# mLSTM decay matrices: the mask from TensorE to GpSimd, the column terms from TensorE to ScalarE's bias

## The chip, the core and the metric

The kernel runs on one core of a Trainium2 chip. A core has five engines that work side by side, each through its own queue of instructions in order: TensorE (PE, matrix products; its weight loads are listed as PEld), VectorE (DVE), ScalarE (ACT), GpSimd (POOL) and SyncE (SP, which here only issues loads and stores). They meet by semaphores. Matrix products write to PSUM, which has eight banks; everything else lies in SBUF. POOL works on SBUF alone. The metric is the time on the device of one execution, in microseconds (us); lower is better.

## The reference, cut to what matters

The reference is one block of a backbone network: a modulation, an input projection whose columns go to four mixers (an mLSTM in both directions, a gated MLP in chunks, a convolution, a state-space scan), an output projection, a layer norm, a SwiGLU feed-forward part and a second layer norm, for 1024 tokens of width 1024 with 256 context tokens. The change touches the mLSTM mixer alone. In a chunk, and for each head and direction, that one computes

```python
logw = jnp.where(lower, b[..., :, None] - b[..., None, :] + ic[..., None, :], -jnp.inf)
m_t = jnp.maximum(inter, jnp.max(logw, axis=-1))
s = jnp.einsum('bhtd,bhsd->bhts', qc, kc) * jnp.exp(logw - m_t[..., None])
num = jnp.einsum('bhts,bhsd->bhtd', s, vc) + w_inter[..., None] * jnp.einsum('bhvk,bhtk->bhtv', C, qc)
```

The factor `exp(logw - m_t)` is the decay matrix. Its exponent is a term that belongs to the later token t, plus a term that belongs to the earlier token s, where s is not after t; elsewhere the factor is zero. In the backward direction the order of the tokens is turned round.

## The kernel before, in words

The kernel is written with a tile framework: the program is traced as Python, and a list scheduler orders the instructions of each engine by its own model of their durations, with the order of tracing as the rank. It puts instructions of a lower rank where it thinks that an engine has nothing else to do. Buffers come from pools with a fixed count for each tag, and an instruction that needs a new buffer waits until an old one is released. On the chip each engine follows the order it was given.

All large products (`projT` and `projK` at L877 and L889, the output projection at L1184, the feed-forward part at L1345 and L1470) are made of three passes in a reduced fp32 format (`fp32r`) with operands that are split into a high and a low part: ACT casts the high part (L854) and DVE makes the remainder (L855).

The mLSTM uses chunks of 128 tokens: 8 for the latent stream and 2 for the context. It has these steps:

- `mlstm_gates` (L374) works on rows that stand for direction, head and chunk: 40 rows for the forward direction from partition 0 and 40 for the backward one from partition 64, each with 128 tokens along the columns. It makes the running sum `b`, the term of the earlier token `av`, its running maximum `A`, the factors of the states and of the denominators (`Q`, transposed at L468 and exponentiated into `G.TW` at L471), and the operands of the decay matrices: `G.R` (`mR`, L463), the row terms -A, spread over four heads, and `G.AL` (`mAL`, L460), the column terms, both as high and low part.
- `mlstm_states` (L475) makes the states of all chunks.
- `mlstm_chunk` (L522) is traced for the chunks 0 to 3 at L1101 and for 4 to 7 at L1135. For each it makes the scores (L531) in two PSUM banks of tag `a`, and for each direction a decay matrix of 128 tokens by 4 heads x 128 tokens: three matmuls into one bank of tag `b` (two buffers), of which the first adds the mask (identity times a table of 0 and -1e30, L538), the second the row terms (`sel1` picks the chunk, L539), and the third the column terms (`sel2` spreads them over a head's columns, L541). ACT takes the exponential of the whole bank into a tile of tag `mD` (L544; three buffers, shared with two other tiles). DVE multiplies it with the scores, half by half (L548), and PE takes the product with the values (L564), again into tag `b`. The rest (L554 to L578) adds the part from the states and divides.
- `mlstm_norm` (L581) is the norm behind it.

While the chunks run, PE's queue holds matmuls of projections (L884, and in the second group L1184 of the output projection's first half) between the short ones, and DVE's queue holds taps of the convolution (`conv_taps`, L675 and L681) and sums of the late modulation (L968). POOL has memsets and a few loads (L1127 and L1128 for the gated MLP's tables). The table of constants `cst` (L756) is loaded once at the start (L840), and L1064 and L1065 cast the identity, `sel1`, `sel2` and both masks into `fp32r`.

Of the kernel before, what the change touches and what calls it, by code (L numbers as in the profile page):

```python
# [9 lines left out]
F32 = mybir.dt.float32  # L10
F32R = mybir.dt.float32r
I32 = mybir.dt.int32
AF = mybir.ActivationFunctionType
ALU = mybir.AluOpType
MUL, ADD, SUB, MAX, MIN = ALU.mult, ALU.add, ALU.subtract, ALU.max, ALU.min
# [4 lines left out]
def bc(ap, shape):  # L20
    return ap.to_broadcast(shape)
# [327 lines left out]
NEG = -1.0e30  # L349
HO = (0, 2, 1, 3)  # L350


def mlstm_consts():

    sel1 = np.zeros((128, 10), np.float32)
    sel2 = np.zeros((128, 40), np.float32)
    dl = np.zeros((128, 4), np.float32)
    rst = np.zeros((128, 104), np.float32)
    for b in (0, 64):
        for h in range(4):  # L360
            for i in range(10):
                r = b + h * 10 + i
                sel1[r, i] = 1
                sel2[r, i * 4 + HO.index(h)] = 1
                dl[r, HO.index(h)] = 1
                if i == 0:
                    rst[:, r] = NEG
    p = np.arange(128)
    mf = np.where(p[:, None] <= p[None, :], 0, NEG).astype(np.float32)
    mb = np.where(p[:, None] >= p[None, :], 0, NEG).astype(np.float32)  # L370
    return {"sel1": sel1, "sel2": sel2, "dl4": dl, "rst": rst, "maskf": mf, "maskb": mb}


def mlstm_gates(e, Gk, page, kp):  # L374

    nc = e.nc
    v, a, pe = nc.vector, nc.scalar, nc.tensor
    G = Env()
    N = 104
# [7 lines left out]
    ps = e.ps("b")  # L387
    for k in range(2):
        for d in range(2):
            pe.matmul(ps[d * 64:d * 64 + 40, k * 128:(k + 1) * 128], lhsT=Gt[:, k, d].rearrange("p h c -> p (h c)"),  # L390
                      rhs=e.ident, start=True, stop=True)
# [48 lines left out]
    nc.gpsimd.memset(Q, 0.0)  # L440
    hl = kp.tile([128, 4, 128], F32R, name="mhl", tag="mD", bufs=3)
    hi, lo, nh, nl = (hl[0:N, i] for i in range(4))
    v.tensor_copy(hi, av)
    v.tensor_tensor(lo, av, hi.bitcast(F32), op=SUB)
    v.tensor_scalar(nh, A, -1.0, None, op0=MUL)
    v.scalar_tensor_tensor(nl, A, -1.0, nh.bitcast(F32), op0=MUL, op1=SUB)
    G.AL, G.R = [], []
    for d in range(2):
        q = slice(d * 64, d * 64 + 40)
        R = (lambda x: x) if d == 0 else (lambda x: x[:, ::-1])  # L450
        v.tensor_scalar(R(Q[q, 0]), av[q], col[q, 0:1], None, op0=ADD)
        v.tensor_scalar(R(Q[q, 1]), A[q], -1.0, col[q, 1:2], op0=MUL, op1=ADD)
        v.scalar_tensor_tensor(R(Q[q, 2]), b[q], -1.0, A[q], op0=MUL, op1=SUB)
        AL = kp.tile([128, 128], F32R, name=f"mAL{d}")
        RR = kp.tile([128, 4, 128], F32R, name=f"mR{d}")
        nc.gpsimd.memset(AL.bitcast(F32), 0.0)
        nc.gpsimd.memset(RR.bitcast(F32), 0.0)
        for x, (s1, s2) in enumerate(((hi, nh), (lo, nl))):
            o = slice(x * 64, x * 64 + 40)
            v.tensor_copy(R(AL[o]), s1[q].bitcast(F32))  # L460
            src = s2[q].bitcast(F32)
            src = src if d == 0 else src[:, ::-1]
            v.tensor_tensor(RR[o], bc(src[:, None, :], [40, 4, 128]), bc(e.dl4[q, :, None], [40, 4, 128]), op=MUL)  # L463
        G.AL.append(AL)
        G.R.append(RR)
    ps = e.ps("b")
    for i in range(3):
        pe.transpose(ps[:, i * N:(i + 1) * N], Q[0:N, i], e.ident[0:N, 0:N])  # L468
    G.TW = kp.tile([128, 3, 2, 40], F32, name="mTW")
# [52 lines left out]
def mlstm_chunk(e, G, c, qT, kT, vx, hb, wp):  # L522
# [10 lines left out]
    D = []  # L533
    for d in range(2):
        i = step(d)
        ps = e.ps("b")
        m = e.mask[:, d, None, :]
        pe.matmul(ps, lhsT=e.identr, rhs=bc(m, [128, 4, 128]), start=True, stop=False)  # L538
        pe.matmul(ps, lhsT=bc(e.sel1[0:104, i:i + 1], [104, 128]), rhs=G.R[d][0:104].rearrange("p h t -> p (h t)"),  # L539
                  start=False, stop=False)  # L540
        pe.matmul(ps, lhsT=G.AL[d][0:104], rhs=bc(e.sel2[0:104, i * 4:i * 4 + 4, None], [104, 4, 128]),  # L541
                  start=False, stop=True)
        D.append(wp.tile([128, 4, 128], F32, name="mD", tag="mD", bufs=3))
        a.activation(D[d].rearrange("p h t -> p (h t)"), ps, AF.Exp)  # L544
    for d in range(2):
# [138 lines left out]
def conv_norm(e, x, y, q, lnw, lnb, wp):  # L684
# [16 lines left out]
    for j in range(2):  # L701
# [9 lines left out]
CST = (("ident", 128), ("jrow", 160), ("dl16", 16), ("dl4", 4), ("rst", 104),  # L711
       ("sel1", 10), ("sel2", 40), ("maskf", 128), ("maskb", 128))

# [49 lines left out]
def body(tc, A, out):  # L763
# [5 lines left out]
    with st:  # L769
# [292 lines left out]
        mp = tc.alloc_tile_pool(name="mixers", bufs=1, side="right", reuse_waits="tile")  # L1062
        cr = mp.tile([128, 434], F32R, name="cr")
        v.tensor_copy(cr[:, 0:128], e.ident)  # L1064
        v.tensor_copy(cr[:, 128:434], cst[:, off["sel1"].start:off["maskb"].stop])  # L1065
        e.identr, e.sel1, e.sel2 = cr[:, 0:128], cr[:, 128:138], cr[:, 138:178]
        e.mask = cr[:, 178:434].rearrange("p (d t) -> p d t", d=2)
        G = mlstm_gates(e, Gk, mp.tile([128, 2080], F32, name="mC", tag="mC"), mp)
# [504 lines left out]
```

## Time and profile before

| | |
|---|---|
| median of 3 runs | 1174.7 us (1173.6 to 1176.86) |
| profiled execution | 1174.02 us, its span 1172.2 us |
| mean granted TensorE clock | 0.989 |
| busy: PE, DVE, ACT, POOL | 97%, 79%, 38%, 1% of the span |
| HBM traffic | 136.54 MB read, 40.35 MB written |

The profile is of one execution. In a row of a group stand the line of the program, the engine, the operation, the tile written and the tiles read, the shape, the count, the busy time in us with the mean duration of one in ns, and the idle time of the engine just before, with what ended it. In a row of a timeline the first two columns are start and length in us, and a bracket holds the idle time before it. Ends of matmuls are modelled, since they are pipelined, so the distance between two starts says more than the length of one. The granted clock is the share of its full clock that TensorE got.

### The profile page before, as it was taken

The numbers are of one execution on the slowest core, as the hardware profiler recorded it, in microseconds if no ns is written. First come the engines' busy times: TensorE is split into PE (matmuls) and PEld (weight loads), VectorE is DVE, ScalarE is ACT, GpSimd is POOL, SyncE is SP. The second block draws the span as 40 slices with busy tenths as digits, with TensorE's granted clock in tenths as the row PEclk, the third lists the DMA queues.
The fourth block names the chain that finished last, engine by engine and source line by source line (L and its number), as shares of the span: only waits on it lengthen the run. The fifth ranks groups of instructions, "written<-read, shape, count | busy, mean of one in ns | idle before, by whom it ended". The sixth has DMA issues, their size and how long they took to land.

```text
span 1172.2 us, 15295 instructions
## 1 busy us (share of the span) xinstructions
PE 1133.1 (97%) x5671; PEld 895.4 (76%) x5671; DVE 930.0 (79%) x1851; ACT 445.6 (38%) x691; POOL 9.6 (1%) x30
## 2 busy tenths in 40 slices
PE   6999999999999999989999999999999999999996
PEld 1487788667888788868887888888887778888884
DVE  6588999978899889879968676777778767766775
ACT  1454444522326433582233332333232336433431
POOL 0010000000000000000000000000000000000000
PEclk9999999999999999999999999999999999999998
DMA  9542111022143346362333545345445679766621
GB/s 359 212 133 89 42 46 57 27 71 70 57 141 109 99 157 212 99 225 73 108 123 112 196 179 180 134 153 192 170 154 202 255 259 349 238 196 220 195 103 72
DMA packets 63147, 177.87 MB, mean 152 GB/s; under 512 B 5537, under 2 KB 9793, under 8 KB 61282
## 3 DMA queue, kind: packets, MB, share of 16 engines
q1 hardware_dynamic: 62658, 175.93, 43.3%
q8 instruction: 44, 0.72, 0.3%
q0 software_dynamic: 272, 0.70, 0.2%
q10 hardware_dynamic: 144, 0.29, 0.1%
q14 instruction: 29, 0.24, 0.1%
HBM read 136.54 MB, written 40.35 MB: 151 GB/s over the span
## 4 chain that ended last, share of the span: by engine, by line
PE 77%; DVE 13%; DMA 4%; issue 4%; ACT 2%; POOL 0%; DVEq 0%; ACTq 0%; POOLq 0%
PE mm L1345 16%; PE mm L884 13%; PE a L1345 8%; PE mm L1470 6%; PE mm L1184 4%; PE b L1345 4%; PE b L884 4%; PE a L1470 3%; PE b L1470 3%; PE mm L893 3%; PE c L1470 2%; PE b L564 1%; DVE whl L855 1%; DVE pg L855 1%; DMA raw<-in_w_dram 1%
## 5 line engine op out<-in xcount | busy, mean ns | idle before, releaser
L854 ACT CAST whl<-raw 128x512 fp32r<-128x512 f32 (+1 forms) x198 | 120.3, 622 | 283.2 <-PE mm L884 69.6
L884 PE MATMUL mm<-pg,whl 128*128 128x512 f32 x816 | 217.7, 406 | 1.4 <-ACT pg L1207 1.2
L1345 PE MATMUL mm<-pg,whl 128*128 128x512 f32 x864 | 205.9, 390 | 0.4 <-DVE whl L855 0.3
L1345 PEld LDWEIGHTS mm<-pg,whl 128*128 128x128 f32 x864 | 161.9, 188 | 35.6 <-issue 0.8
L884 PEld LDWEIGHTS mm<-pg,whl 128*128 128x128 f32 x816 | 147.7, 190 | 38.8 <-issue 6.1
L855 DVE TENSOR_TENSOR whl<-raw,whl 128x512 fp32r<-128x512 f32 (+1 forms) x198 | 133.6, 689 | 46.3 <-ACT whl L854 44.7
L1345 PE MATMUL a<-pg,whl 128*128 128x512 f32 x432 | 104.7, 390 | 3.6 <-ACT whl L854 3.6
L1345 PEld LDWEIGHTS a<-pg,whl 128*128 128x128 f32 x432 | 80.7, 188 | 21.3 <-ACT whl L854 4.8
L855 DVE TENSOR_TENSOR pg<-raw,pg 128x1024 fp32r<-128x1024 f32 (+1 forms) x52 | 59.6, 1149 | 20.8 <-ACT pg L854 20.7
L855 DVE TENSOR_TENSOR pg<-whl,pg 128x1024 fp32r<-128x1024 f32 (+1 forms) x42 | 47.4, 1133 | 31.9 <-ACT pg L854 31.6
L854 ACT CAST pg<-raw 128x1024 fp32r<-128x1024 f32 (+1 forms) x52 | 51.5, 992 | 48.9 <-DMA raw<-in_w_dram 18.0
L854 ACT CAST pg<-whl 128x1024 fp32r<-128x1024 f32 (+1 forms) x42 | 41.1, 980 | 65.9 <-PE c L1470 25.2
L893 PE MATMUL mm<-whl,pg 128*128 128x256 f32 (+1 forms) x448 | 63.1, 288 | 0.0
L893 PEld LDWEIGHTS mm<-whl,pg 128*128 128x128 f32 x448 | 58.1, 190 | 1.5 <-issue 1.1
L1345 PE MATMUL b<-pg,whl 128*128 128x512 f32 x216 | 51.9, 389 | 0.0
L1184 PE MATMUL mm<-pg 128*128 128x512 f32 x192 | 50.8, 409 | 0.0
L1184 PE MATMUL mm<-whl,pg 128*128 128x512 f32 x192 | 50.2, 398 | 0.3 <-DVE pg L1172 0.3
L1470 PE MATMUL mm<-pg,pg 128*128 128x512 f32 x171 | 48.0, 389 | 0.0
L1470 PE MATMUL a<-pg,pg 128*128 128x512 f32 x162 | 47.2, 390 | 0.2 <-DVE hs L1484 0.2
L1470 PE MATMUL b<-pg,pg 128*128 128x512 f32 x162 | 47.1, 389 | 0.0
L1345 PEld LDWEIGHTS b<-pg,whl 128*128 128x128 f32 x216 | 40.5, 188 | 8.4
L1184 PEld LDWEIGHTS mm<-pg 128*128 128x128 f32 x192 | 37.4, 198 | 8.6 <-DVE pg L855 0.7
(468 smaller groups left out, 1838.2 us busy)
## 6 DMA issues: line engine op xcount, KB each, us to landing
raw<-in_w_dram SPq DMA_DIRECT2D x59, 512.0 KB
gd<-pg SPq DMA_DIRECT2D x22, 1024.0 KB
whl<-gd SPq DMA_DIRECT2D x35, 512.0 KB
pg<-in_w2k_dram SPq DMA_DIRECT2D x11, 1024.0 KB
td<-pg SPq DMA_DIRECT2D x11, 1024.0 KB
raw<-td SPq DMA_DIRECT2D x20, 512.0 KB
pg<-in_wm_dram SPq DMA_DIRECT2D x16, 512.0 KB
raw<-in_wo_dram SPq DMA_DIRECT2D x16, 512.0 KB
```

Of the source, the lines that this page charges most:

```text
L564: pe.matmul(ps[:, x * 65:(x + 1) * 65], lhsT=D[d][:, x], rhs=vx[:, h, :], start=True, stop=True)
L854: a.copy(hi, r)
L855: v.tensor_tensor(lo, r, hi.bitcast(F32), op=SUB)
L884: pe.matmul(ps[h], lhsT=W(wi, k), rhs=rhs(hi, h, k), **f)
L893: pe.matmul(ps, lhsT=lhs(hi, k), rhs=Ws[k // 4](wi, k % 4), start=(k == 0 and n == 0), stop=(k == 7 and n == 2))
L1184: pe.matmul(ps, lhsT=Yr(hi, half, k)[:, t * 128:(t + 1) * 128], rhs=Ws[k // 2](wi, k % 2), start=(i + n == 0), stop=(i == 7 and n == 2))
L1345: pe.matmul(ps, lhsT=W[:, wi, k, :], rhs=B[b][hi][:, k], start=(first and k + n == 0), stop=(k == 3 and n == 2), skip_group_check=True)
L1470: pe.matmul(ps[t], lhsT=Ag[:, hi, k, t * 128:(t + 1) * 128], rhs=Bg[:, wi, k], start=(first and k0 + k + m == 0), stop=(k0 + k == NK - 1 a ...
```

## The change

The mask and the column terms leave TensorE. The kernel after keeps one matmul for a decay matrix, that of the row terms. `mlstm_gates` no longer makes the split column terms; it turns `av` back into the order of the tokens, in the place of the gate inputs (`IF`), transposes it with the three others, and copies the result into `G.a`, where the tokens stand on partitions. In `mlstm_chunk` ACT takes the exponential for each head by itself, 128 columns with the head's column of `G.a` as bias. Then POOL's `affine_select` goes over the whole matrix in place, and puts zero where the earlier token is not before or at the later one. The tables `sel2`, `maskf` and `maskb` go from the constants, and with them the casts.

```diff
-    hl = kp.tile([128, 4, 128], F32R, name="mhl", tag="mD", bufs=3)
-    hi, lo, nh, nl = (hl[0:N, i] for i in range(4))
-    v.tensor_copy(hi, av)
-    v.tensor_tensor(lo, av, hi.bitcast(F32), op=SUB)
+    hl = kp.tile([128, 2, 128], F32R, name="mhl", tag="mD", bufs=3)
+    nh, nl = (hl[0:N, i] for i in range(2))
...
-        AL = kp.tile([128, 128], F32R, name=f"mAL{d}")
+        v.tensor_copy(R(IF[q, 0]), av[q])
         RR = kp.tile([128, 4, 128], F32R, name=f"mR{d}")
-        nc.gpsimd.memset(AL.bitcast(F32), 0.0)
         nc.gpsimd.memset(RR.bitcast(F32), 0.0)
-        for x, (s1, s2) in enumerate(((hi, nh), (lo, nl))):
+        for x, s2 in enumerate((nh, nl)):
             o = slice(x * 64, x * 64 + 40)
-            v.tensor_copy(R(AL[o]), s1[q].bitcast(F32))
...
-    for i in range(3):
-        pe.transpose(ps[:, i * N:(i + 1) * N], Q[0:N, i], e.ident[0:N, 0:N])
+    for i in range(4):
+        pe.transpose(ps[:, i * N:(i + 1) * N], Q[0:N, i] if i < 3 else IF[0:N, 0], e.ident[0:N, 0:N])
+    G.a = kp.tile([128, 2, 40], F32, name="mAL")
+    for d in range(2):
+        v.tensor_copy(G.a[:, d], ps[:, 3 * N + d * 64:3 * N + d * 64 + 40])
...
-        m = e.mask[:, d, None, :]
-        pe.matmul(ps, lhsT=e.identr, rhs=bc(m, [128, 4, 128]), start=True, stop=False)
         pe.matmul(ps, lhsT=bc(e.sel1[0:104, i:i + 1], [104, 128]), rhs=G.R[d][0:104].rearrange("p h t -> p (h t)"),
-                  start=False, stop=False)
-        pe.matmul(ps, lhsT=G.AL[d][0:104], rhs=bc(e.sel2[0:104, i * 4:i * 4 + 4, None], [104, 4, 128]),
-                  start=False, stop=True)
+                  start=True, stop=True)
         D.append(wp.tile([128, 4, 128], F32, name="mD", tag="mD", bufs=3))
-        a.activation(D[d].rearrange("p h t -> p (h t)"), ps, AF.Exp)
+        for x, h in enumerate(HO):
+            a.activation(D[d][:, x], ps[:, x * 128:(x + 1) * 128], AF.Exp, bias=G.a[:, d, h * 10 + i:h * 10 + i + 1])
+
+        nc.gpsimd.affine_select(D[d], D[d], pattern=[[0, 4], [1 - 2 * d, 128]], compare_op=ALU.is_ge, fill=0.0, base=0,
+                                channel_multiplier=2 * d - 1)
...
-       ("sel1", 10), ("sel2", 40), ("maskf", 128), ("maskb", 128))
+       ("sel1", 10))
...
-        cr = mp.tile([128, 434], F32R, name="cr")
-        v.tensor_copy(cr[:, 0:128], e.ident)
-        v.tensor_copy(cr[:, 128:434], cst[:, off["sel1"].start:off["maskb"].stop])
-        e.identr, e.sel1, e.sel2 = cr[:, 0:128], cr[:, 128:138], cr[:, 138:178]
-        e.mask = cr[:, 178:434].rearrange("p (d t) -> p d t", d=2)
+        e.sel1 = mp.tile([128, 10], F32R, name="cr")
+        v.tensor_copy(e.sel1, cst[:, off["sel1"]])
```

More of the change, by code (lines that the diff above doesn't have):

```diff
@@ L355, in mlstm_consts @@
     sel1 = np.zeros((128, 10), np.float32)
-    sel2 = np.zeros((128, 40), np.float32)
     dl = np.zeros((128, 4), np.float32)
@@ L363, in mlstm_consts @@
                 sel1[r, i] = 1
-                sel2[r, i * 4 + HO.index(h)] = 1
                 dl[r, HO.index(h)] = 1
@@ L367, in mlstm_consts @@
                     rst[:, r] = NEG
[L368 to L371, printed above, removed]
+    return {"sel1": sel1, "dl4": dl, "rst": rst}
 def mlstm_gates(e, Gk, page, kp):
@@ L440, in mlstm_gates @@
     nc.gpsimd.memset(Q, 0.0)
-    hl = kp.tile([128, 4, 128], F32R, name="mhl", tag="mD", bufs=3)
-    hi, lo, nh, nl = (hl[0:N, i] for i in range(4))
-    v.tensor_copy(hi, av)
-    v.tensor_tensor(lo, av, hi.bitcast(F32), op=SUB)
+    hl = kp.tile([128, 2, 128], F32R, name="mhl", tag="mD", bufs=3)
+    nh, nl = (hl[0:N, i] for i in range(2))
     v.tensor_scalar(nh, A, -1.0, None, op0=MUL)
     v.scalar_tensor_tensor(nl, A, -1.0, nh.bitcast(F32), op0=MUL, op1=SUB)
-    G.AL, G.R = [], []
+    G.R = []
     for d in range(2):
@@ L463, in mlstm_gates @@
             v.tensor_tensor(RR[o], bc(src[:, None, :], [40, 4, 128]), bc(e.dl4[q, :, None], [40, 4, 128]), op=MUL)
-        G.AL.append(AL)
         G.R.append(RR)
     ps = e.ps("b")
-    for i in range(3):
-        pe.transpose(ps[:, i * N:(i + 1) * N], Q[0:N, i], e.ident[0:N, 0:N])
+    for i in range(4):
[3 more added lines that the diff above has]
+        v.tensor_copy(G.a[:, d], ps[:, 3 * N + d * 64:3 * N + d * 64 + 40])
     G.TW = kp.tile([128, 3, 2, 40], F32, name="mTW")
```

## The prediction

> **What bounds the kernel now.** I read the busy shares first, then the windows, the chain of waits, and last the timeline of the stages in which the decay matrices are made.
>
> ```profile
> PE 1133.1 (97%) x5671; PEld 895.4 (76%) x5671; DVE 930.0 (79%) x1851; ACT 445.6 (38%) x691; POOL 9.6 (1%) x30
> ```
>
> A busy PE need not be PE at its pace, so the stages decide. The next rows are those of the gates (222 to 245), the chunks 0 to 3 (272 to 303), what follows them, the chunks 4 to 7 (366 to 409), and two short stretches; the columns are length, busy us and count of PE, PEld, DVE, ACT and POOL, granted clock, DMA share and GB/s.
>
> ```profile
> 222.00:245.00 23.00, 21.82 (x96) 16.04 (x95) 20.19 (x63) 9.39 (x17) 1.81 (x5) 0.93 0.16 58
> 239.50:242.50 3.00, 3.00 (x8) 2.42 (x8) 2.88 (x12) 0.00 (x0) 0.00 (x0) 0.50 0.00 0
> 272.00:303.00 31.00, 31.00 (x194) 24.92 (x193) 27.37 (x85) 8.80 (x15) 0.00 (x0) 1.00 0.13 41
> 303.00:365.00 62.00, 61.21 (x383) 54.24 (x382) 56.99 (x119) 21.96 (x33) 0.00 (x0) 1.00 0.29 94
> 366.00:409.00 43.00, 40.58 (x321) 31.77 (x318) 37.33 (x112) 22.92 (x30) 0.00 (x0) 0.97 0.39 128
> 407.00:413.00 6.00, 6.00 (x19) 5.03 (x19) 2.93 (x14) 0.72 (x2) 0.00 (x0) 0.50 0.89 285
> ```
>
> PE has no idle time in the first chunk stage and 2.4 us in the second; DVE is busy for 27.37 of 31 and 37.33 of 43 us, so it stands close behind. POOL does nothing in either. Twice the granted clock is 0.50, and both times PE had just waited. The second of these waits is in the timeline of PE:
>
> ```profile
> 402.53 0.51 PE L1184 MATMUL mm<-pg 128*128 128x512 f32 x1
> 404.59 1.33 PE L564 MATMUL b<-vx,mD 128*128 128x65 f32 x8 [1.56 <-DVE mD L548]
> ```
>
> The chain of waits shows what a 512-column matmul costs where PE runs through, and what the slow clock costs:
>
> ```profile
> 305.58 8.92 PE mm L884 x39
> 406.69 1.87 PE b L564 x8
> 408.56 9.06 PE mm L1184 x29
> ```
>
> 39 matmuls in 8.92 us are 0.229 us each. The 29 behind the wait took 9.06 instead of 6.64 us, so that wait cost 1.56 us of idle time and 2.4 us or more of slow clock. So PE bounds these stages, with DVE the engine that makes it wait. Any time taken from PE there should move everything behind it forward: the out-projection and the feed-forward part are ordered by PE and by buffers that come free after it.
>
> **The change part by part.** *Two matmuls go from every decay matrix.* Eight chunks by two directions are 16 matrices, so 32 matmuls of 512 columns and their weight loads go. Their places in the second chunk:
>
> ```profile
> 279.68 0.51 PE L538 MATMUL b<-cr 128*128 128x512 f32 x1
> 280.02 0.39 PE L539 MATMUL b<-mR,cr 104*128 104x512 f32 x1
> 280.25 0.38 PE L541 MATMUL b<-cr,mAL 104*128 104x512 f32 x1
> 280.47 0.41 PE L538 MATMUL b<-cr 128*128 128x512 f32 x1
> 280.71 0.40 PE L539 MATMUL b<-mR,cr 104*128 104x512 f32 x1
> 280.95 0.38 PE L541 MATMUL b<-cr,mAL 104*128 104x512 f32 x1
> 281.16 0.63 PE L884 MATMUL mm<-pg,whl 128*128 128x512 f32 x2
> ```
>
> From start to start they stand 0.21 to 0.24 us apart (the 0.34 after the first is the change from short matmuls, which stays). 32 x 0.229 = 7.3 us, with ends of 32 x 0.21 = 6.7 and 32 x 0.24 = 7.7.
>
> *The exponential becomes four.* The row of today's exponential, and the nearest for 128 columns, and for the price of a bias column the same 512 columns with and without one:
>
> ```profile
> L544 ACT ACTIVATE mD<-b 128x512 f32<-128x512 f32 x16 | 9.2, 596 | 12.6 <-PE b L541 12.3
> L324 ACT ACTIVATE s5Yg<-a 128x128 f32<-128x128 f32 x16 | 3.1, 284 | 3.0 <-PE a L321 3.0
> L345 ACT ACTIVATE s5sg<-b,cols 128x512 f32<-128x512 f32 x4 | 2.7, 687 | 3.5 <-PE b L342 3.5
> L1057 ACT ACTIVATE pg<-mm 128x512 f32<-128x512 f32 x16 | 9.4, 598 | 16.5 <-PE mm L884 16.4
> L702 ACT ACTIVATE ap<-c,cols 128x256 f32<-128x256 f32 x8 | 4.1, 560 | 10.1 <-PE c L700 10.1
> ```
>
> A bias adds 687 - 598 = 89 ns, so one of 128 columns takes about 373 ns. Eight of L702 take 4.1 us of busy time where 8 x 560 ns are 4.5, which is the overlap of pairs, some 0.1 us. Four in a row then take 373 + 3 x 0.28, about 1.2 us, and a matrix has its exponentials 0.6 us later; ends are 4 x 0.284 - 0.596 = 0.5 without any bias price and 4 x 0.373 - 0.596 = 0.9 without overlap. ACT gains 8 x 0.6 = 5 us of work in each chunk stage, against 22 and 20 us of room there. Queued behind these activations stand the casts of weights (L854), for which DVE's remainder (L855) and then a PE group wait; they are made ahead of use, so I cost this at nothing, and at up to 0.6 us per cast that PE does wait for.
>
> *The mask becomes a select on POOL.* No row shows one. The rows that POOL has:
>
> ```profile
> L457 POOL MEMSET mR<- 128x512 f32 x2 | 1.1, 532 | 0.0
> L1028 POOL MEMSET ap<- 128x3072 f32 x1 | 2.7, 2667 | 4.2 <-DVE pg L922 4.2
> 252.41 0.54 POOL L1128 DMA_DIRECT2D gbs<-in_sgu_bb_dram  x1 [28.01 <-DVE mC L494]
> ...
> L675 DVE SCALAR_TENSOR_TENSOR cp<-ap,wc,cp 128x528 f32<-128x528 f32 x9 | 6.8, 753 | 0.0
> L673 DVE TENSOR_SCALAR cxn<-ap,wc 128x512 f32<-128x512 f32 x1 | 0.5, 482 | 0.0
> ```
>
> A memset of the same 512 columns only writes: 0.53 us is the low end. The longest instruction POOL has, 2.67 us, is the high end. I take 0.85 us, near the low end because the shape is the same, and more than it because the select also reads: on DVE (last two rows) a step that reads two tensors takes some 1.5 times one that reads one. Nothing else is queued on POOL in these stages; its last issue, L1128, is at 252. Behind the select waits DVE's product with the scores (L548), and behind that in DVE's queue the rest of the chunk and the conv taps (L675); for L548 PE waits at L564.
>
> The Trainium skill, "GPSIMD Engine Reference", section on elementwise cycle accounting, has 1.03 to 2.6 cycles per element at 1.2 GHz, by which the select would be an estimated 0.44 to 1.1 us; the sum below would stay as it is within half a microsecond. No run here shows it yet.
>
> *The chain of a matrix* is thus longer by 0.6 + 0.85 + about 0.1 for one more handover, 1.6 us. How much PE sees of that depends on what stands between L539 and L564 in PE's order. Today's waits in this place:
>
> ```profile
> L564 PE MATMUL b<-vx,mD x128: 217/275/447, 275.8 to 408.1; 128*128 128x65 f32 x128
> ...
>   PEld b L564: 2.4, 4
>   PE b L564: 1.6, 1
> ```
>
> Five waits in 16 matrices, 4.0 us. The list scheduler lays projection matmuls (L884, L1184) between, and lays more where it counts on a longer chain, and there are enough: the second stage stands in front of all of the out-projection's first half. If the five places that show today get 0.5 us more each, that is 2.5 us; the ends are 0 (all covered, or the one long wait is gone: first rival) and 6.5 (second rival).
>
> *Gates.* DVE loses two casts of constants, the two halves of the column term and four copies into mAL, and gains two copies of 40x128 and two of 128x40 from PSUM; PE gains one transpose.
>
> ```profile
> L460 DVE CAST mAL<-mhl x4: 189/221/223, 236.2 to 237.7; 40x128 fp32r<-40x128 f32 x4
> ...
> 239.05 0.46 PE L431 MATMUL b<-mC,oz 1*128 1x104 f32 x2 [0.91 <-ACT mC L424]
> ```
>
> By the L460 row the four copies that come cost what the four that go cost, 0.2 us each; the casts and the two halves are four more, some 0.9 us of DVE. Only what stood before the wait of 0.91 us can help PE. I take -0.2, with ends of -1.0 and +0.3 (a transpose and two copies late). The two memsets of mAL on POOL go for nothing.
>
> *Constants.* 296 of 718 columns of the table go, 148 of the row's 359 KB:
>
> ```profile
> cst<-in_cst_dram SPq DMA_DIRECT2D x1, 359.0 KB
> 8.20 0.20 DVE L1042 TENSOR_SCALAR wc<-wc 128x62 f32<-128x62 f32 x1 [3.44 <-DMA wc<-in_conv_t_dram]
> ```
>
> The load queue has it ahead of other loads, but DVE, on which the start hangs, waits for another queue's load. I take 0; without that cover it would be some 0.4 us gained.
>
> **Sum.** -7.3 - 0.2 + 2.5 = -5.0 us. The profiled execution took 1174.02 us (span 1172.2, 1.8 outside); that becomes 1169.0. It lies 0.7 us under the median of the runs, 1174.7, so for the median I say **1169.7**.
>
> **Rivals.** *More than PE's part.* The new order removes the wait at 402.5 and with it the slow clock: 1.56 + 2.4 + about 0.8 (eight L564 in 1.87 us, which take about 1.0 at full clock) = 4.8 us beside 7.5, so 1162.4. For it: the wait is one single place, and the longer chain calls for more matmuls between. Against it: the wait is DVE's lateness in its own order (L576 and others ahead of L548), which the change does not cure.
>
> *The saving goes into waits.* In the second stage the eight matrices are not covered by 0.6 us each (4.8 us), and one more slow-clock stretch, as long as that at 239.5, costs about 1.7 us: 7.5 - 6.5 = 1.0 gained, 1173.7. For it: the second stage shows waits already. Against it: the first shows nearly none.
>
> *DVE is held up by POOL, slower.* In both stages each select keeps DVE from its next instruction that reads two tensors from SBUF, for the select's own length.
>
> ```profile
> L576 DVE TENSOR_TENSOR mt<-mtmp,mr 128x512 f32<-128x512 f32 x3 | 2.1, 685 | 0.0
> ```
>
> Eight selects of 0.85 us are 6.8 us of DVE in each stage. Its room shrinks with PE's time: 31.0 - 27.4 - 3.65 = 0 in the first and 43.0 - 37.3 - 3.65 = 2.0 in the second. So the first stage gets 6.8 - 3.65 = 3.15 longer than before, the second 6.8 - 2.0 - 3.65 = 1.15; with the gates' -0.2 and one slow-clock stretch of 1.7, +5.8: 1180.5. It decides from 16 d = 7.5 + 2.0 without that stretch, a loss of d = 0.6 us per select. For it: DVE's room, and L675 and L576 are such instructions, the first of them its filler. Against it: the taps are of low rank and can go to the stage behind (57.0 of 62 us busy), and no row shows POOL slowing DVE, though none could: POOL only writes today. The Trainium skill, "SBUF — State Buffer", section on SBUF's two sides, states such an exclusive lock between GpSimd and a DVE instruction with two SBUF inputs; this rival is what it would do here at its worst.
>
> That the change does not do what it says, because the scheduler lays the matmuls elsewhere, would show as other counts; that 32 matmuls go is certain.
>
> **How the numbers follow.** Forecast 0.45 (its own range 1167.2, no added waits, to 1172.7), more 0.13, waits 0.23, DVE held up 0.19. A measurement of this kernel tells about 0.3% (3.5 us) from no change: 0.05 of the forecast lies within that. Faster 0.40 + 0.13 = 0.53, within 0.05 + 0.23 = 0.28, slower 0.19. The range goes from the first rival to the last, 1162 to 1180.5; a select near 2.67 us would lie beyond it.
>
> **What would show it.** 31 matmuls fewer on PE (32 go, a transpose comes), 5640, and 7 us less PE work up to the end of the second stage; four rows of about 373 ns for one of L544; the select's own row between 0.53 and 2.67 us; waits of L564 of 4 to 7 us in all; DVE's L675 and L576 at 753 and 685 ns still. Longer DVE rows beside POOL, or stretches at clock 0.50 in 272 to 303, would prove the forecast wrong, and so would a gain that is there at 409 and gone at 512.

## The result and the profile after

The kernel after took 1192.03 us (median; 1186.11 to 1195.45), the kernel before 1175.65 us beside it: a ratio of 1.0136 (95% interval 1.0088 to 1.0184). The forecast was 1169.7 us, its range ended at 1180.5. The change costs some 16 us where 5 were to be gained. The profiled execution took 1194.38 us. One execution of e8 below ran at a mean granted clock of 0.77 and took 1375.56 us; the median given for e8 leaves it out.

The head of the page of the kernel after; the counts are as forecast, and the span is not:

```profile
span 1192.7 us, 15335 instructions
...
PE 1147.2 (96%) x5640; PEld 898.0 (75%) x5640; DVE 931.3 (78%) x1848; ACT 467.2 (39%) x749; POOL 21.1 (2%) x44
```

31 matmuls fewer are busy for 14 us longer. Where the time comes in shows when the same instructions are followed through both traces. Starts in us, with the line numbers of the kernel before:

| first or last start | before | after | after minus before |
|---|---|---|---|
| out-projection, first L1184 | 369.71 | 367.77 | -1.9 |
| last chunk, last L564 | 408.14 | 425.68 | +17.5 |
| out-projection, last L1184 | 496.28 | 505.04 | +8.8 |
| feed-forward, first L1345 | 598.83 | 609.62 | +10.8 |
| feed-forward, last L1345 | 947.16 | 964.14 | +17.0 |
| down projection, last L1470 | 1160.54 | 1180.89 | +20.4 |

The 17.5 us at the last chunk shrink to 8.8 because PE had by then already issued 96 of the out-projection's 384 matmuls, where the kernel before had issued 39 at its last chunk. So there are two losses, far from each other: one in the second group of chunks, and one of some 9 us in a part that the change does not touch at all.

**The first loss.** The windows of the kernel after; the columns are those of the prediction's windows:

```profile
272.00:303.00 31.00, 30.75 (x193) 23.57 (x194) 26.59 (x72) 12.07 (x28) 2.86 (x4) 1.00 0.18 58
...
382.00:410.00 28.00, 25.13 (x147) 19.38 (x146) 15.39 (x43) 14.32 (x27) 2.54 (x4) 0.70 0.17 57
...
436.00:475.00 39.00, 35.00 (x151) 28.50 (x150) 33.78 (x57) 12.80 (x16) 0.00 (x0) 0.87 0.53 172
...
388.50:405.50 17.00, 16.14 (x87) 12.17 (x88) 7.96 (x22) 7.70 (x16) 1.91 (x3) 0.51 0.18 63
453.20:463.20 10.00, 7.82 (x22) 6.51 (x23) 8.37 (x11) 1.57 (x2) 0.00 (x0) 0.50 0.57 179
```

The same windows of the kernel before, and what it did in 388 to 405:

```profile
382.00:410.00 28.00, 25.58 (x189) 20.29 (x186) 23.66 (x74) 12.44 (x17) 0.00 (x0) 0.94 0.31 99
...
436.00:475.00 39.00, 38.48 (x181) 31.45 (x180) 36.73 (x59) 12.56 (x17) 0.00 (x0) 1.00 0.62 196
...
388.00:405.00 17.00, 14.59 (x124) 10.97 (x122) 14.46 (x44) 7.74 (x10) 0.00 (x0) 1.00 0.30 103
```

The first group (272 to 303) is as full as before. In 382 to 410 PE issues 147 matmuls in place of 189, at a granted clock of 0.70 in place of 0.94, and in the 17 us from 388.5 on it runs at half clock: 87 matmuls for 124. DVE is busy for 15.4 us in place of 23.7, so DVE is not what bounds it. What DVE waits for stands in the timeline of ACT:

```profile
376.89 1.28 ACT L534 ACT_TABLE_LOAD   x1
378.19 0.37 ACT L534 ACTIVATE mD<-b,mAL 128x128 f32<-128x128 f32 x1
378.56 1.28 ACT L695 ACT_TABLE_LOAD   x1
379.85 1.02 ACT L695 ACTIVATE ap<-c,cols 128x256 f32<-128x256 f32 x2
380.89 1.28 ACT L534 ACT_TABLE_LOAD   x1
382.19 0.37 ACT L534 ACTIVATE mD<-b,mAL 128x128 f32<-128x128 f32 x1
...
383.39 0.37 ACT L534 ACTIVATE mD<-b,mAL 128x128 f32<-128x128 f32 x1
383.78 1.28 ACT L619 ACT_TABLE_LOAD   x1
385.07 0.20 ACT L619 ACTIVATE cmv<-cmv 128x2 f32<-128x2 f32 x1
385.29 1.28 ACT L534 ACT_TABLE_LOAD   x1
386.59 0.88 ACT L534 ACTIVATE mD<-b,mAL 128x128 f32<-128x128 f32 x3
```

and behind it in those of POOL and PE:

```profile
387.07 0.64 POOL L536 TENSOR_SCALAR_AFFINE_SELECT mD<-mD 128x512 f32<-128x512 f32 x1 [16.93 <-ACT mD L534]
```

```profile
386.71 0.63 PE L693 MATMUL c<-cst,cxn 128*128 128x128 f32 x4 [1.13 <-DVE cxn L689]
388.22 1.97 PE L557 MATMUL b<-vx,mD 128*128 128x65 f32 x8 [0.88 <-DVE mD L541]
...
392.95 1.98 PE L640 MATMUL c<-gw,pg 128*64 128x128 f32 x16 [0.85 <-DVE gwl L643]
...
453.32 1.84 PE L974 MATMUL c<-oz,macc 128*128 128x1 f32 x8 [1.52 <-DVE macc L961]
457.22 5.06 PE L1174 MATMUL mm<-whl,pg 128*128 128x512 f32 x11 [2.06 <-DVE pg L1162]
```

An exponential that was one instruction could not be interrupted. Its four parts can: the scheduler put the SiLU of the convolution (L695) and the square root of a norm (L619) between them, and each of these changes of function loads a table for 1.28 us. A matrix whose four parts need 1.2 us gets its first part at 378.2 and its last at 386.6. Two of the 16 matrices are torn by table loads in this way, both of the second chunk of this group. There are 45 such loads in the whole kernel, where before there were 35. PE waits about a microsecond three times, and then runs at half clock. The whole group ends late, and so the chunks' tail falls among the late modulation and the out-projection, where PE waits again (453, 457) and the clock drops for another 10.2 us.

**The second loss.** The feed-forward matmuls, in a stretch of 250 us in which PE has no idle time worth telling. First the kernel before, then the kernel after; the count is what matters:

```profile
650.00:900.00 250.00, 248.72 (x1095) 205.04 (x1094) 1.00 0.48 173
```

```profile
650.00:900.00 250.00, 250.00 (x1083) 203.21 (x1082) 1.00 0.47 172
```

The clock is 1.00 in both and the code is the same, yet fewer matmuls fit: 250 us over 1083 are 0.2308 us each, over 1095 they are 0.2283 (with 1.3 us of waits in it). From the first to the last of this line it takes 354.5 us in place of 348.3.

### The profile page after: what moved, and what is told of

It is laid out like the page before. It is cut to its first block, busy times and chain, and to the rows that moved or that the text cites. A ratio compares the mean times of both kernels' runs of the same rounds, so it can differ in the third digit from the quotient of the medians.

```text
span 1192.7 us, 15335 instructions
## 1 busy us (share of the span) xinstructions
PE 1147.2 (96%) x5640; PEld 898.0 (75%) x5640; DVE 931.3 (78%) x1848; ACT 467.2 (39%) x749; POOL 21.1 (2%) x44
## 4 chain that ended last, share of the span: by engine, by line
PE 84%; DVE 9%; ACT 3%; DMA 2%; issue 1%; POOL 0%; DVEq 0%; ACTq 0%; POOLq 0%
PE mm L1335 16%; PE mm L877 15%; PE a L1335 8%; PE mm L1174 6%; PE mm L1460 6%; PE a L1460 5%; PE b L1335 4%; PE b L1460 4%; PE b L877 4%; PE mm L886 3%; PE c L1460 2%; PE b L557 1%; DVE whl L848 1%; PE c L814 1%; PE b L287 1%
## 5 line engine op out<-in xcount | busy, mean ns | idle before, releaser
L1335 PE MATMUL a<-pg,whl 128*128 128x512 f32 x432 | 107.8, 397 | 3.6 <-ACT whl L847 3.6
L886 PEld LDWEIGHTS mm<-whl,pg 128*128 128x128 f32 x448 | 58.3, 190 | 1.6 <-issue 1.1
L1174 PE MATMUL mm<-whl,pg 128*128 128x512 f32 x192 | 51.2, 413 | 3.1 <-DVE pg L1162 2.7
L1174 PE MATMUL mm<-pg 128*128 128x512 f32 x192 | 49.1, 400 | 0.5 <-ACT pg L847 0.5
L1174 PEld LDWEIGHTS mm<-whl,pg 128*128 128x128 f32 x192 | 37.4, 199 | 12.4 <-DVE pg L1162 3.2
```

Of the source, the lines that this page charges most:

```text
L886: pe.matmul(ps, lhsT=lhs(hi, k), rhs=Ws[k // 4](wi, k % 4), start=(k == 0 and n == 0), stop=(k == 7 and n == 2))
L1174: pe.matmul(ps, lhsT=Yr(hi, half, k)[:, t * 128:(t + 1) * 128], rhs=Ws[k // 2](wi, k % 2), start=(i + n == 0), stop=(i == 7 and n == 2))
L1335: pe.matmul(ps, lhsT=W[:, wi, k, :], rhs=B[b][hi][:, k], start=(first and k + n == 0), stop=(k == 3 and n == 2), skip_group_check=True)
```

## The experiments

Three causes were on trial: the Exps that are torn apart (A), the select between the Exp and its product (B), and the shorter table of constants, which moves every tile behind it in SBUF by 296 x 4 = 1184 bytes in each partition (C). In each diff only the core stands. Medians are in us, and each ratio is to the kernel before on the same chip, with its 95% interval.

**The change again, and with the old addresses.** e1 is the kernel after, unchanged. e2 adds unused columns in place of those that went:

```diff
-       ("sel1", 10))
+       ("sel1", 10), ("pad", 296))
```

> The changed kernel itself, once more, beside the kernel before on the same chip. Its loss has two parts by the traces: about 11 us between the start of the second chunk group (367) and the end of the output projection (505), and about 9 us behind 540, where no instruction was changed and the matmuls of the feed-forward part stand 0.231 us apart in place of 0.227. If the second part belongs to this kernel (its buffers lie elsewhere in SBUF, since the table of constants is 1184 bytes per partition shorter), it comes again: 1186 to 1195 us and 0.231 us. If it belongs to the chip or the hour, the time is about 1183 and the pace as in the kernel before.

> The changed kernel with 296 unused columns at the end of the table of constants, so that the tiles behind it lie where they lay before. Theory of the addresses: the feed-forward matmuls are 0.227 us apart again, and the time is about 9 us under that of the changed kernel, some 1183. Theory of chip or hour: pace and time as in the changed kernel on the same chip. The chunk stages, with the exponentials torn apart by other functions (45 table loads), stay as they are by both.

e1: 1189.14, ratio 1.0142 (1.0107 to 1.0177). e2: 1180.38, ratio 1.0049 (1.0027 to 1.0071). Unused columns gain 8.8 us. The feed-forward line takes 348.0 us in e2 and 354.6 in e1, the down projection 211.6 and 213.2, and the second group of chunks ends at 425.4 and 425.5: the padding cures the second loss and leaves the first.

**Which property of the address.** e6 adds 8 unused columns (32 bytes) to the kernel before, e7 adds 8 and e9 adds 104 to the kernel after (e9 with e4's edit below):

```diff
-       ("sel1", 10), ("sel2", 40), ("maskf", 128), ("maskb", 128))
+       ("sel1", 10), ("sel2", 40), ("maskf", 128), ("maskb", 128), ("pad", 8))
```

> The kernel before with 8 unused columns at the end of its constants table, so that every tile behind it begins 32 bytes further in each partition, and nothing else changed. The change moved them by 1184 bytes, which is 18.5 times 64. Theory C1 (the pace of the feed-forward matmuls hangs on where in a block of 64 bytes the operands begin): first to last matmul of that part takes 354.5 us in place of 348, 0.231 us from one to the next from 500 us on, and the time is 1181 to 1185 us. Theory C2 (it hangs on something else of the place, as the distance between two tiles or which stretch of memory they lie in): 348 us, and 1174 to 1176 us.

> The kernel after with 8 unused columns behind its shorter constants table: every tile behind it begins 1152 bytes (18 times 64) earlier than in the kernel before, in place of 1184. Theory C1 (place in a block of 64 bytes): the feed-forward part takes 348 us, as with 296 columns, and the time is about 1180.5 us (1178 to 1183). Theory C2 (another property of the place): it stays at 354.5 us, and the time is 1187 to 1191 us.

> The kernel after, its four Exps at high priority, with 104 unused columns of constants in place of 296: the tiles behind the table begin 768 bytes earlier than in the kernel before. In the runs so far a 512-column matmul of the feed-forward part took 0.233 to 0.234 us where the place of the rows that it reads and that of the weights loaded for the next one differ modulo 256 bytes, and 0.2267 where they agree. Theory C3 (that is what decides, with 256 as the modulus): 768 is 3 x 256, so the two agree again: 348 us from the first to the last matmul of that part, and 1174 to 1179 us, as with 296 columns. If the distance has to be one of a larger modulus, or the absolute place counts: 353 to 355 us and 1183 to 1187 us. The page that holds the addresses is the program's own list of where it puts its tiles.

e6: 1181.61, ratio 1.0059 (1.0032 to 1.0087): 32 bytes of unused constants, and nothing else, cost the kernel before about 6 us. e7: 1187.59, ratio 1.0118 (1.0079 to 1.0158). C1's figures came true for e6 (354.4 us for the line), but not its reason, the 64-byte block: e7 restores the place in such a block and stays slow. Sorted by where the operands lie, the starts of the matmuls gave the next guess. The program's list of addresses puts eight of the tiles that hold the rows at places that never move, and the weights (`whl`) at places that move with the constants. PE loads the weights of the next matmul while it streams the rows of the present one, and D is the distance between the places of these two, modulo 256 bytes, the shorter way round. (In the trace of the kernel before, a weight load of 188 ns starts 3 ns after the start of the matmul ahead of its own, by the medians of L1345.) Mean distance from one start to the next in us, for L1345, with the count in brackets:

```
             D = 0                D not 0
before       0.2269 (1499)        -
e2           0.2269 (1501)        -
e6           0.2283  (641)        0.2334 (861), D = 32
e7           0.2280  (642)        0.2329 (861), D = 128
after        0.2279  (642)        0.2340 (861), D = 96
e9           0.2269 (1503)        -
```

861 x (0.2340 - 0.2269) is 6.1 us, nearly the whole of the 6.2. No larger modulus shows: in the kernel before, the distances take all eight multiples of 256 below 2048, some 187 matmuls each, at 0.2266 to 0.2274 us. The down projection tells the next weights from a matmul's own, which agree in place with its rows throughout: only where it switches between two places does D differ from 0, 120 times in the kernel after, e6 and e7 together. 100 of these take 0.2328 to 0.2353 us in the mean, 20 in the kernel after 0.2282, where the kernel before takes 0.2267. e9 was the test of this rule, with addresses that no kernel had had: 768 bytes away, 3 x 256. It took 1176.81, ratio 1.0023 (1.0006 to 1.0039), as e4 did with 296 columns, and 347.8 us for the line. In 250 us, e6, e7 and e9:

```profile
650.00:900.00 250.00, 248.81 (x1076) 201.62 (x1075) 1.00 0.47 171
```

```profile
650.00:900.00 250.00, 250.00 (x1086) 203.42 (x1085) 1.00 0.48 173
```

```profile
650.00:900.00 250.00, 248.81 (x1098) 205.59 (x1097) 1.00 0.49 174
```

Groups of twelve in the timeline of e6 show both kinds side by side, rows at places that stay (here the groups that write banks `a` and `b`) and rows that move with the weights (here the group that writes `mm`): 2.80 us from start to start for the first, 2.75 for the second. In the kernel before, below it, twelve take 2.72.

```profile
703.39 2.96 PE L1345 MATMUL a<-pg,whl 128*128 128x512 f32 x12
706.19 2.91 PE L1345 MATMUL mm<-pg,whl 128*128 128x512 f32 x12
708.94 2.96 PE L1345 MATMUL b<-pg,whl 128*128 128x512 f32 x12
```

```profile
704.34 2.88 PE L1345 MATMUL b<-pg,whl 128*128 128x512 f32 x12
707.06 2.88 PE L1345 MATMUL mm<-pg,whl 128*128 128x512 f32 x12
```

**The mask alone, and the Exps together.** e3 is the kernel before with the mask moved to the select, one Exp and the column terms on TensorE. e4 is e2 with the four Exps at high priority:

```diff
-        m = e.mask[:, d, None, :]
-        pe.matmul(ps, lhsT=e.identr, rhs=bc(m, [128, 4, 128]), start=True, stop=False)
...
+        nc.gpsimd.affine_select(D[d], D[d], pattern=[[0, 4], [1 - 2 * d, 128]], compare_op=ALU.is_ge, fill=0.0, base=0,
+                                channel_multiplier=2 * d - 1)
```

```diff
+            with e.tc.high_priority():
+                a.activation(D[d][:, x], ps[:, x * 128:(x + 1) * 128], AF.Exp, bias=G.a[:, d, h * 10 + i:h * 10 + i + 1])
```

> The kernel before with the mask alone moved: TensorE keeps the row and column terms, ScalarE one exponential of 512 columns for a matrix, GpSimd the select; the constants are as before. Theory A (the loss in the second chunk group comes from the four exponentials that the scheduler tears apart): no such loss, 16 matmuls fewer at 0.229 us, so about 3.7 us under the kernel before, 1171 to 1174. Theory B (the select holds up VectorE, or its step in the chain makes TensorE wait): slower than before by 3 us or more, with longer rows for VectorE instructions that read two tensors from SBUF.

> e2 with the exponentials of a matrix at high priority, so that the scheduler keeps most of them together; the order has 42 table loads in place of 45, and the second chunk group has no group of four torn apart. Theory A: the loss of the second chunk group goes, so about 8 to 10 us under e2, about 1172. Theory B: as e2 within 2 us.

e3: 1179.59, ratio 1.0063 (1.0040 to 1.0085), with 16 matmuls fewer. e4: 1176.56, ratio 1.0018 (0.9997 to 1.0040). With the Exps kept together the median is 3.8 us under e2's, between the two expectations (42 table loads for 45; the half clock from 392.5 on lasts 10.2 in place of 17.1 us). That is not clear of the spread: e2's executions go from 1174.79 us at a mean granted clock of 0.989 to 1183.27 us at 0.980, the profiled one among the longest with 1182.85, and e4's go from 1173.83 to 1179.69. The select by itself loses. What PE waits for in e4 and e3, in that order:

```profile
392.28 1.71 PE L558 MATMUL b<-vx,mD 128*128 128x65 f32 x8 [2.59 <-DVE mD L542]
```

```profile
405.82 0.50 PE L1184 MATMUL mm<-pg 128*128 128x512 f32 x1 [3.46 <-DVE pg L1172]
```

In e4 the product itself is late. In e3 PE waits longest for other work of DVE, which the new order had put there and which was late.

**The Exps alone.** e5 keeps the mask on TensorE and moves only the column terms: four Exps with a bias, no select, 16 matmuls fewer. e12 is the same kernel again.

```diff
+        m = e.mask[:, d, None, :]
+        pe.matmul(ps, lhsT=e.identr, rhs=bc(m, [128, 4, 128]), start=True, stop=False)
...
-        nc.gpsimd.affine_select(D[d], D[d], pattern=[[0, 4], [1 - 2 * d, 128]], compare_op=ALU.is_ge, fill=0.0, base=0,
-                                channel_multiplier=2 * d - 1)
```

> The kernel before with the column terms alone moved: four Exps with a bias for each matrix, TensorE keeps the mask and the row terms (so 16 matmuls fewer than before, not 32), no select on GpSimd, constants as wide as before. Saved on TensorE: 16 x 0.229 = 3.7 us. Theory A (the four Exps: they hold ScalarE longer, and other functions' table loads come between them, so that the products are late in the second group of chunks): in that group, 382 to 410 us, TensorE waits and then runs at half clock for 10 us or more, as with the whole change padded, and the time is 1177 to 1182 us. Theory B (it is the select on GpSimd between the Exp and the product that is late): that group goes as before, its last matmul of exponentials and values ends by 408 us, and the time is 1170 to 1173 us. In both the 512-column matmuls of the feed-forward part stand 0.2267 us apart after 500 us.

> The kernel of e5 a second time, to learn whether it is below the kernel before: 16 matmuls fewer (3.7 us of TensorE), four Exps in place of one, no select, tiles where they were. If its gain is real, the ratio to the kernel before is 0.996 to 0.999 and the median 1171 to 1174 us; if e5's 1172.65 was chance, the ratio is 0.999 to 1.001 with 1 inside its interval.

e5: 1172.65, ratio 0.9983 (0.9963 to 1.0004). e12: 1171.04, ratio 0.9948 (0.9925 to 0.9972). e5's interval still holds 1; e12's does not, and its ratio lies a little below the 0.996 to 0.999 expected. This part of the change is a gain of 2.5 to 5.5 us by the two medians, around the 3.7 that its matmuls are worth, so the four Exps in themselves cost nothing that can be measured. Theory A has to be put more narrowly: not four Exps, but four Exps with another function between them. Here the order happens to keep them whole (eight in a row, and 40 table loads), and DVE and PE go as before:

```profile
381.35 2.17 ACT L539 ACTIVATE mD<-b,mAL 128x128 f32<-128x128 f32 x8
```

```profile
382.00:410.00 28.00, 25.36 (x195) 20.32 (x192) 24.60 (x77) 17.04 (x35) 0.00 (x0) 0.94 0.38 124
```

**A select that nobody waits for.** e10 is e5 with 16 selects of the same size into a spare buffer; the order on PE, ACT and DVE is that of e5.

```diff
+        z = wp.tile([128, 520], F32, name="mz", tag="mtmp", bufs=2)[:, 0:512].rearrange("p (h t) -> p h t", h=4)
+        nc.gpsimd.affine_select(z, G.R[d].bitcast(F32), pattern=[[0, 4], [1 - 2 * d, 128]], compare_op=ALU.is_ge, fill=0.0, base=0,
+                                channel_multiplier=2 * d - 1)
```

> The kernel of e5 (four Exps with a bias, mask and row terms on TensorE, 1172.65 us) with 16 selects of the same size on GpSimd that write a spare buffer which nobody reads; the buffer is one of the two that take a chunk's numerators in turn, so that the selects fall between the chunks. The order on TensorE, ScalarE and VectorE is the same as in e5. Theory B1 (the select costs because it stands in the chain from the Exp to the product): the time stays at 1171 to 1174.5 us. Theory B2 (GpSimd's select holds up VectorE wherever it runs, my third rival of the prediction): 1176 to 1181 us, with VectorE's instructions longer by 4 us or more in all.

1175.81, ratio 1.0006 (0.9991 to 1.0020): between the two expectations, 3.2 us over e5 and just outside what B1 allows; its interval overlaps e5's (0.9963 to 1.0004) and lies clear of e12's (0.9925 to 0.9972). The trace shows a part of it. DVE with the selects (e10), then the same instructions without them (e5):

```profile
300.04 0.85 DVE L577 TENSOR_TENSOR mC<-mt 128x256 f32<-128x256 f32 x1
300.81 1.12 DVE L674 SCALAR_TENSOR_TENSOR cxn<-ap,wc,cxn 128x512 f32<-128x512 f32 x1
```

```profile
300.05 0.42 DVE L574 TENSOR_TENSOR mC<-mt 128x256 f32<-128x256 f32 x1
300.38 0.74 DVE L671 SCALAR_TENSOR_TENSOR cxn<-ap,wc,cxn 128x512 f32<-128x512 f32 x1
```

Both read two tensors from SBUF, and both ran while POOL was at two selects (299.53 to 301.39). Beside the 16 selects nine rows of DVE are longer than in e5, by 3.0 us in all, of which 2.7 are in rows that read two tensors from SBUF, and the stretch at half clock behind the chunks is 6.8 us in place of 3.4. So holding up DVE is part of the select's price, whether or not a product waits for the select.

**Two attempts at a better version.** e8 makes a chunk's matrices while the chunk before it still divides; e11 uses the select in the first four chunks only:

```diff
+    Dn = mlstm_mats(e, G, c + 1, wp) if more else None
     r = wp.tile([128, 2, 2, 2], F32, name="mr")
```

```diff
-        m = e.mask[:, d, None, :]
-        pe.matmul(ps, lhsT=e.identr, rhs=bc(m, [128, 4, 128]), start=True, stop=False)
+        if c > 3:
+            m = e.mask[:, d, None, :]
+            pe.matmul(ps, lhsT=e.identr, rhs=bc(m, [128, 4, 128]), start=True, stop=False)
...
+        if c < 4:
+            nc.gpsimd.affine_select(D[d], D[d], pattern=[[0, 4], [1 - 2 * d, 128]], compare_op=ALU.is_ge, fill=0.0, base=0,
```

> The kernel after with 296 unused columns of constants and its four Exps at high priority (1176.6 us), and the matrices of a chunk now made while the chunk before it still computes its quotient, in three buffers of their own, with one left for the temporaries that shared those. If the lateness of the matrices at their products is what costs the second group (theories A and B), the waits of TensorE between 382 and 410 us fall below 3 us in all, its clock there stays up longer, and the time is 1171 to 1175 us. If the loss is in what ScalarE and VectorE then do later (its queue as such), it is 1176 to 1180 us. The single buffer for the temporaries can cost some 2 us.

> The kernel of e5 with the mask moved to the select in the first four chunks alone (their Exps at high priority), where the runs showed a gain of 2 to 4 us, and left on TensorE in the last four, where they showed a loss: 24 matmuls fewer than before, 5.5 us of TensorE. If a select costs only where its matrix is awaited (theory B1): 1169 to 1172.5 us, below e5 and below the kernel before. If it costs everywhere: 1174 to 1178 us.

e8: 1176.94, ratio 1.0013 (0.9993 to 1.0033), no better than e4: one wait of 4.77 us for a product (L564, at 402) took the place of the others. e11: 1174.39, ratio 0.9993 (0.9982 to 1.0005), above the 1169 to 1172.5 expected and just inside the 1174 to 1178 of a select that costs everywhere. It decides for neither: its second group has no select, yet that group ended 9.2 us later than e5's (414.55 for 405.34): the new order had torn its Exps again,

```profile
383.17 1.66 ACT L541 ACTIVATE mD<-b,mAL 128x128 f32<-128x128 f32 x6
384.85 1.28 ACT L627 ACT_TABLE_LOAD   x1
386.15 0.20 ACT L627 ACTIVATE cmv<-cmv 128x2 f32<-128x2 f32 x1
386.37 1.28 ACT L541 ACT_TABLE_LOAD   x1
387.66 0.37 ACT L541 ACTIVATE mD<-b,mAL 128x128 f32<-128x128 f32 x1
```

and PE waited 1.38 us and ran at half clock for 6.8. That was not the question of e11, but it shows the tearing of theory A in a group without any select.

## Why the prediction was wrong

Laid end to end, the runs go from the kernel before to the kernel after like this:

| step | runs | us |
|---|---|---|
| column terms to the bias (16 matmuls less) | before to e5, e12 | -2.5, -5.5 |
| mask to the select (16 matmuls less) | e5 to e4 | +3.9 |
| Exps torn apart | e4 to e2 | +3.8 |
| tiles moved by 1184 bytes | e2 to e1 | +8.8 |
| all | before to e1 | +14.1 |

With e5 the four sum to 14.0, since each step starts where the last ended. (e5 ran on another chip than e4, e2 and e1; the kernel before took 1175.17 us beside it and 1175.04 beside them.) The third row is the weakest, since the executions of e4 and e2 overlap. A sum that does not close by itself: the select costs 3.9 + 3.7 = 7.6 us when its 16 matmuls are put back, and e3, which has no bias, gives 1179.59 - 1175.04 + 3.7 = 8.2; from e12 in place of e5 it would be 5.5 + 3.7 = 9.2.

*Two matmuls go from every matrix, -7.3.* Right: 5640 matmuls, and the out-projection, which has the first 16 of the 32 ahead of it (3.65 us), starts 1.9 us earlier in the kernel after and 4.4 in e4.

*Gates, -0.2.* Nothing is late here. In the kernel after PE issues 99 matmuls in this stretch where it issued 96, at a granted clock of 1.00 in place of 0.93; the stretch at half clock behind the wait of 0.91 us is gone, which the term did not count.

```profile
222.00:245.00 23.00, 21.65 (x99) 15.78 (x98) 20.41 (x57) 10.11 (x16) 1.53 (x3) 1.00 0.17 58
```

*The exponential becomes four.* The price of one was right (373 ns forecast, 370 the median), and so was that of four in a row (1.2 us forecast; eight take 2.17 in e5). The sentence that failed is "they are made ahead of use, so I cost this at nothing". It looked at what stands behind the Exps in ACT's queue, and not at what can come between them. L544 had three table loads in the kernel before, for 16 Exps: a sign in the old profile that other functions lay close by, and that a gap between two Exps costs 1.28 us twice. The kernel after has nine. The rows of before and of after:

```profile
L544 ACT ACT_TABLE_LOAD x3 | 3.8, 1283 | 0.6 <-PE b L541 0.6
...
L534 ACT ACT_TABLE_LOAD x9 | 11.5, 1283 | 3.7 <-PE b L530 3.5
```

*The mask becomes a select.* The tile view of the kernel after:

```profile
L534 ACT ACTIVATE mD<-b,mAL x64: 357/370/421, 278.9 to 421.7; 128x128 f32<-128x128 f32 x64
...
L536 POOL TENSOR_SCALAR_AFFINE_SELECT mD<-mD x16: 631/636/1508, 280.1 to 422.2; 128x512 f32<-128x512 f32 x16
...
  PE b L557: 1.7, 5
  PEld b L557: 1.6, 2
```

0.636 us for 0.85 taken, inside its ends of 0.53 and 2.67. The estimate from the Trainium skill ("GPSIMD Engine Reference", the section on elementwise cycle accounting) was 0.44 to 1.1 us; the trace agrees by this median, and its longest select, 1.508 us beside DVE, lies above. The failed step is the price for PE: "If the five places that show today get 0.5 us more each, that is 2.5 us". The waits at this place did not grow at all, 3.3 us in the kernel after for 4.0 before. They came elsewhere, at products of other parts (L693, L640, L974, L1174) that DVE reached later, and most of the price was the clock behind them: 17.1 and 10.2 us at half clock from 388 and 453 on, where the kernel before had 6.8 from 407 on. I priced a longer chain at its own consumer; a list of fixed order passes the delay to whatever stands next.

*The slow clock.* I gave it 1.7 to 2.4 us for one stretch. The stretches inside the runs last 3.4, 6.8, 10.2 and 17.1 us, and one of 17.1 costs 37 matmuls of mixed sizes (87 for 124). The Trainium skill ("TensorE: Matmul & The Clock Gate", Part 1) has a window of about 3.4 us after which the clock changes; the steps of the lengths agree with it. What I missed is that one stretch can be five such steps long. It does not need waits for that: of the 17.1 us only the first 6.8 hold one (0.85 us), and from 395.08 to 405.32 PE is busy without a gap, mostly with matmuls of 65 to 130 columns, and still at half clock. What keeps the clock down there is open.

*Constants, 0.* This is the largest miss, 8.8 us. I priced the load of the table and never asked where its 1184 bytes lay. The bound should have named the address of every tile behind it, in the parts that are all TensorE.

*Rivals.* The third, DVE held up by POOL, came nearest in sign, and its mechanism is there: in the kernel after L961 takes up to 1.12 us beside a select. In e3 even the rows that the rival named, L675 and L576, take up to 1.12 us beside one. But it acts at 0.1 to 0.2 us for each select (over 16 selects 1.8 us in the kernel after, 3.0 in e10 and 3.4 in e3), not 0.6 and more, and not in the first group of chunks, which it should have hit hardest and which was as full as before. The second rival said that the saving goes into waits and one more slow stretch in the second group; that is the place, but 7.6 + 3.8 = 11.4 us where it had 6.5. No rival had the addresses. Of the signs named, longer DVE rows beside POOL came, and stretches at half clock in 272 to 303 did not; "a gain that is there at 409 and gone at 512" did not come: at 409 the loss was already there.

*What stays open.* How the select's 7.6 us divide between its place in the chain and DVE's lock: by the ratios e10 stands 2.7 us over e5 and 6.8 over e12, and its trace shows 3.0 us of longer DVE rows and 3.4 us more at half clock. And the pairs with D = 0 are slower too in the kernels that have the others (0.2279 for 0.2269, and 0.2286 for 0.2267 in the down projection of the kernel after). Their extra time lies right behind pairs with D not 0: in both parts of the kernel after, e6 and e7 the first three of them take 0.228 to 0.234 us in the mean, and from the tenth on they take 0.227, as in the kernel before. Why it lasts for some matmuls, no run tells.

## What to carry to other kernels

Before an instruction is cut in pieces, look at what else is in its engine's queue: pieces can be torn apart, and on ACT each tear between two functions cost two table loads of 1.28 us here; put them at one priority or check the order. Removing a buffer or a table moves every tile behind it, so a change of size is an experiment on all matmuls that follow: compare the distance of starts in a part that was not touched, and put the bytes back before judging the rest. Of this change, the half that moves the column terms to the bias is worth keeping (ratio 0.9948, and 0.9983 with 1 inside its interval); the mask is cheaper on TensorE, where it was.

## What the runs showed of the hardware

- A 128x512 matmul of this kernel takes 0.233 to 0.234 us from start to start where the rows it streams and the weights loaded meanwhile differ in place modulo 256 bytes, and 0.227 where they agree: 2.6 to 3.1%, at a granted clock of 1.00. Distances of 32, 96 and 128 bytes were all slow; weights moved by 768 bytes, a multiple of 256, were as fast as unmoved ones. Right behind slow ones some matmuls with no distance are slow as well. The Trainium skill ("TensorE: Matmul & The Clock Gate", the step-by-step section of Part 2) says that loading the next weights takes no read bandwidth from the running matmul. In these runs the pace of the matmuls hangs on where the weights loaded meanwhile lie, so the two are not free of each other, and the measurement decides. That the two reads meet in the memory is the likely reason, but it is argued, not shown.
- An affine select of 128x512 in fp32 on POOL takes 0.636 us by itself, and up to 1.5 us in the kernel after (2.23 in e4) while DVE works. DVE rows beside one get longer too (0.42 to 0.85 us, 0.74 to 1.12 us).
- A stretch at half clock can go on without any wait of PE: 10.2 of the 17.1 us from 388.25 on in the kernel after.
